# A hand-written TensorE order for the even layer's preparation, with attention one phase earlier

## The chip, the cores and the metric

The kernel runs on one core of a Trainium2 chip. The metric is device time in microseconds of one execution; the median of three timed runs stands for a kernel. A profiled execution gives the trace.

## The reference, cut to what matters

A decoder trunk of two layers: 256 positions, width 2048, float32. Only the even layer's mixer is touched here.

```python
h = x @ e_w_in                                   # even layer: one combined projection
ha, hq, hk, hv = split(h)
ya = rwkv7_mix(ha, ...)                          # A: 16 heads of 64
yb = swa_sink_attention(rot(q), rot(k), v, sinks)  # B: window 128, 16 query / 2 key heads of 64
mix = concatenate([ya, yb]) @ e_w_out
x = layer_norm(alpha * x + mix); x = layer_norm(alpha * x + swiglu(x)); x = x + sigmoid(x Wg) * (p Wp)

def rwkv7_mix(h, ...):
    h = h + (token_shift(h) - h) * mu
    r, k, v, lw, la, lg = split(h)               # widths 3 x 1024, 64, 64, 160
    decay = exp(-exp(-softplus(-(w0 + tanh(lw) @ w_up)) - 0.5))
    a = sigmoid(a0 + la @ a_up); g = sigmoid(lg) @ g_up
    kk = k * k_k / max(norm(k * k_k), 1e-12)     # per head
    # per position: state = state * w + (state @ -kk) (kk*a)^T + v k^T ;  y = state @ r
    y = groupnorm(y) * gn_w + gn_b + bonus;  return y * g

def swa_sink_attention(q, k, v, sinks):          # softmax over 128 keys back, with a sink logit per head
    e = exp(s - m); prob = e / (sum(e) + exp(sink - m)); return prob @ v
```

The odd layer (differential attention), both feed-forward blocks and the gates follow; their instructions are the same in both kernels.

## The kernel before, in words

Every product of activations and weights is three matmuls: a weight tile is read by DMA (`raw`), ACT rounds it to `hi` (L151), DVE subtracts to get `lo` (L152), and TensorE adds hi·xh, lo·xh and hi·xl into PSUM. `gemm_steps` (matmuls L178 to L180, 512 columns) yields after every six matmuls, so other work can be put between. `gemm_t` (L201 to L205, 256 columns) gives the transposed form and yields nothing.

The even mixer runs through these stages. **Preparation** (`wkv_operands`): x is transposed (L216) and split (L222, L223); a projection to 288 columns feeds the low-rank products for decay, rate and gate (L586, L590, L591, L625); then, for each half of the heads, keys and receptances are projected, and small float32 products (L633, L651, L660, L689, L697) with VectorE work in between make the recurrence operands `ar` and `bk` of all heads. From L730 to L746 VectorE inverts all 32x32 triangles of the recurrence, with two dependent instructions in each of 30 steps (L739, L741). The first value projection, `values(0, pr)`, and the attention's keys and first queries (`swa_project`) come from `gemm_steps` and lie beside the inverse. Here the Tile scheduler chooses the order on every engine.

**Phases 1 to 4** (`even_layer`): the order on TensorE is that of the program (`manual_schedule`). `weave` advances two units of the recurrence in turn, each `unit(g, c)` being four heads and half of the positions; with every link of a unit it advances the `side` work by a rate. The sides are: phase 1 `values(1, pp)`, phase 2 the second half of the queries (`swa`), phase 3 a part of the output projection with attention of head pairs 0 to 3, phase 4 another part with head pairs 4 to 7. A unit starts with four first products (L789) that are yielded as one link, each masked by VectorE into `lmat` (L790); triangular solves follow (L800 to L841); its post chain (L878 to L891) on ACT, VectorE and POOL turns `py` into the group-normed, gated result. A head pair of attention goes through scores (L964), maximum and bias on VectorE (L966), exponentials on ACT (L975), division (L980), transposes of the probabilities (L989) and the product with the values (L995). Its PSUM tiles `sx` come from a pool of two. Behind phase 4 the last output projection closes the mixer.

TensorE, VectorE and ACT each work through their own list in order; an instruction that waits holds up all that stands behind it on its engine. In phases 1 to 4 the lists of VectorE and ACT are still the Tile scheduler's.

Of the kernel before, what the change touches and what calls it, by code (L numbers as in the profile page):

```python
# [80 lines left out]

def take(steps, n):

    for _ in range(n):
        if next(steps, 0) == 0:
            return
        yield


class Trunk:  # L90
# [16 lines left out]
    def psum(self, mm, sm, sx=0):  # L107

        ctx = ExitStack()
        pool = lambda n, b: ctx.enter_context(self.tc.tile_pool(name=n, bufs=b, space=PSUM, reuse_waits="tile"))  # L110
        self.mm, self.sm = pool("mm", mm), pool("sm", sm)
        self.sx = pool("sx", sx) if sx else self.sm
        return ctx
# [70 lines left out]
    def gemm_t(self, lhs, view, n0, widths):  # L184
# [7 lines left out]
        for j, (xh, xl) in enumerate(lhs):  # L192
            hi, lo = next(ws)
            for kk in range(2):
                k = 2 * j + kk
                f0 = 0
                for i, w in enumerate(widths):
# [8 lines left out]
                                     skip_group_check=True)  # L206
        return [acc[i // 2][:w, i % 2] for i, w in enumerate(widths)]
# [203 lines left out]
def even_layer(T, a, src):  # L411
# [4 lines left out]
    with ExitStack() as ctx:  # L416
        ev = ctx.enter_context(tc.tile_pool(name="ev", bufs=1, reuse_waits="tile"))
        with tc.tile_pool(name="prep", bufs=1) as pr, T.psum(4, 4):
            ops, xT, values = wkv_operands(T, src, w_in, a, ev, pr)
            y = ops[-2]  # L420
        with tc.tile_pool(name="pairs", bufs=2, reuse_waits="tile") as pp, T.psum(2, 4, 2):
# [6 lines left out]
            swa = swa_project(T, pp, xT, w_in, a)  # L428
            qkv = next(swa)
            while next(swa) is None:  # L430
                pass
# [58 lines left out]
def wkv_operands(T, src, w_in, a, ev, pr):  # L490
    tc, nc = T.tc, T.nc
    xT = []

    def incoming():

        x = [T.res.tile([P, D], F32, name=f"x{t}") for t in range(NT)]
        for j in range(8):
# [11 lines left out]
    nc.vector.memset(vec, 0.0)  # L509
# [7 lines left out]
    nc.sync.dma_start(out=vec[50:51, 0:32], in_=mu[3328:3360].rearrange("(n p) -> n p", p=32))  # L517
    vps = T.sm.tile([P, 64], F32, name="s")
# [11 lines left out]
    early = tc.tile_pool(name="early", bufs=1)  # L530
    er = early.__enter__()
    gup0 = er.tile([P, AW], F32, name="gup0")
    gup1 = er.tile([32, AW], F32, name="gup1")
    nc.sync.dma_start(out=gup0, in_=a["e_g_up"][0][0:128])
    nc.sync.dma_start(out=gup1, in_=a["e_g_up"][0][128:160])
# [23 lines left out]
    for i in range(2):  # L559
        nc.vector.tensor_tensor(out=cum[:, i], in0=cum[:, i], in1=half, op=ALU.subtract)  # L560
# [8 lines left out]
    lg0 = er.tile([P, SEQ], F32, name="lg0")  # L569
    lg1 = er.tile([32, SEQ], F32, name="lg1")  # L570
    mix(ps[0], P, MU_L, lm)
    mix(ps[1], P, MU_L + 1, lg0)
    mix(ps[2], 32, MU_L + 2, lg1)
    nc.scalar.activation(out=lm[0:64], in_=lm[0:64], func=AF.Tanh)
    nc.scalar.activation(out=lg0, in_=lg0, func=AF.Sigmoid)
    nc.scalar.activation(out=lg1, in_=lg1, func=AF.Sigmoid)
# [3 lines left out]
    for c in range(2):  # L580
        cs = slice(c * 512, (c + 1) * 512)
        w0 = T.row(a["e_w0"][0], c * 512, 512, "brow", pr, 2)
        for t in range(NT):
            ts = slice(t * P, (t + 1) * P)
            z = T.sm.tile([P, 512], F32, name="s")
            nc.tensor.matmul(z, lm[0:64, ts], ups[0:64, cs], start=True, stop=True)  # L586
            nc.vector.tensor_tensor(out=sig[t][:, cs], in0=z, in1=w0, op=ALU.add)
            nc.scalar.activation(out=sig[t][:, cs], in_=sig[t][:, cs], func=AF.Sigmoid)
            g = T.sm.tile([P, 512], F32, name="s")
            nc.tensor.matmul(g, lg0[:, ts], gup0[:, cs], start=True, stop=False)  # L590
            nc.tensor.matmul(g, lg1[:, ts], gup1[:, cs], start=False, stop=True)  # L591
            nc.scalar.copy(out=gate[t][:, cs], in_=g)
    early.__exit__(None, None, None)
    T.rotary_tables(a["positions"][0])


    late = tc.tile_pool(name="late", bufs=1, reuse_waits="tile")
    lt = late.__enter__()
# [6 lines left out]
    for b in range(4):  # L605
        nc.vector.tensor_copy(out=m32[32 * b:32 * b + 32], in_=mtri[32 * b:32 * b + 32, 32 * b:32 * b + 32])
# [6 lines left out]
    ft = lambda n: lt.tile([P, SEQ], F32, name=n, bufs=4)  # L613
    bs = [ev.tile([P, AH], F32, name=f"bs{t}") for t in range(NT)]
    for c in range(2):
        k, kk, av, rks = [], [], [], []
        ps = T.gemm_t(xT, w_in, AW + c * 512, [128] * 4)
        for i in range(4):
            k.append(ft("k"))
            mix(ps[i], P, MU_K + 4 * c + i, k[i])  # L620
        ss = T.sm.tile([8, SEQ], F32, name="s")
        for i in range(4):
# [3 lines left out]
            av.append(ft("a"))  # L626
            nc.scalar.activation(out=av[i], in_=pa, func=AF.Sigmoid, bias=col[:, A0 + f:A0 + f + 1])
            kk.append(ft("kk"))
            nc.vector.tensor_scalar(out=kk[i], in0=k[i], scalar1=col[:, KK + f:KK + f + 1], scalar2=None,
                                    op0=ALU.mult)  # L630
            sq = lt.tile([P, SEQ], F32, name="sq")
            nc.scalar.activation(out=sq, in_=kk[i], func=AF.Square)
            nc.tensor.matmul(ss, sel[:, i], sq, start=i == 0, stop=i == 3)  # L633
        inv = lt.tile([8, SEQ], F32, name="inv")
        s0 = lt.tile([8, SEQ], F32, name="s0")
        s1 = lt.tile([8, SEQ], F32, name="s1")
        nc.vector.tensor_scalar(out=s1, in0=ss, scalar1=1e-30, scalar2=None, op0=ALU.max)
        nc.scalar.activation(out=s0, in_=s1, func=AF.Sqrt)
        nc.vector.reciprocal(out=inv, in_=s0)
        nc.vector.tensor_tensor(out=inv, in0=inv, in1=s1, op=ALU.mult)  # L640
        nc.vector.tensor_tensor(out=s0, in0=s0, in1=inv, op=ALU.add)
        nc.vector.tensor_scalar(out=s0, in0=s0, scalar1=0.5, scalar2=1e-12, op0=ALU.mult, op1=ALU.max)
        nc.vector.reciprocal(out=inv, in_=s0)

        pr_ = T.gemm_t(xT, w_in, c * 512, [128] * 4)
        for i in range(4):
            f = 4 * c + i
            r = lt.tile([P, SEQ], F32, name="r", bufs=2)
            mix(pr_[i], P, MU_R + f, r)
            pi = T.sm.tile([P, SEQ], F32, name="s")  # L650
            nc.tensor.matmul(pi, selT[:, i], inv, start=True, stop=True)  # L651
            bv = lt.tile([P, SEQ], F32, name="b", bufs=2)
# [6 lines left out]
            for t in range(NT):  # L659
                nc.tensor.matmul(pc[:, t], sig[t][:, f * P:(f + 1) * P], cum, start=True, stop=True)  # L660
# [236 lines left out]
def swa_project(T, pool, xT, w_in, a):  # L897
# [32 lines left out]
    for c in range(2):  # L930
# [16 lines left out]
        if c == 0:  # L947
            yield True
# [295 lines left out]
```

## Time and profile before

| quantity | value |
|---|---|
| median of three runs | 2599.96 us (2599.18 to 2602.28) |
| profiled execution, its span | 2597.83 us, 2595.9 us |
| mean granted TensorE clock | 0.993 of full |
| VectorE, ACT busy | 57%, 44% of the span |
| even mixer up to the last attention | 0 to 474.8 us of the span |

Busy time overlaps between instructions of one engine that are pipelined, so the length of a stretch is taken from starts and not from a sum of lengths. [...] The stages of the table of rows below were cut at the first matmul behind the x transposes (10.65 us), the end of the low-rank projection (33.5), the start of the inverse (199), and the first products of the phases.

### The profile page before, as it was taken

The page shows a single profiled execution, that of the slowest core. Times are in us where ns is not written, and L with a number is a line of the kernel's source. Part 1 is how long each engine was busy: PE and PEld are TensorE (multiplying, and loading weights), DVE is VectorE, ACT ScalarE, POOL GpSimd, SP SyncE. Part 2 cuts the span into 40 slices and gives each one's busy share as a digit, 9 for nine tenths or more (in the row PEclk, how much of TensorE's full clock was granted, in tenths as well). Part 3 has the DMA queues.
Part 4 walks back from the last instruction along what each step waited for, and adds up shares of the span by engine and source line. Part 5 has one row for each costly group of instructions (what it writes and reads, how often), then busy time and mean ns, then how long its engine had stood idle before and what let it go on. Part 6 is the DMA issues. An engine that isn't in the chain of part 4 may idle for free.

```text
span 2595.9 us, 32573 instructions
## 1 busy us (share of the span) xinstructions
PE 2541.7 (98%) x12509; PEld 2083.3 (80%) x12509; DVE 1478.8 (57%) x2144; ACT 1140.3 (44%) x1508; POOL 60.3 (2%) x126
## 2 busy tenths in 40 slices
PE   8999989999999999999999999999999999999999
PEld 6887766778888888888888888887888888888877
DVE  4668556774544454455756666657454444445574
ACT  5563344444444344443444444435444334444343
POOL 0002110000000000000000000000000000000000
PEclk9999989999999999999999999999999999999999
DMA  6445322666666666666666555557666666666654
GB/s 190 129 119 170 106 66 74 199 208 190 187 190 191 194 197 187 189 189 192 201 193 193 170 171 168 165 171 220 193 187 188 193 194 194 187 189 188 193 179 159
DMA packets 240858, 458.56 MB, mean 177 GB/s; under 512 B 15345, under 2 KB 21155, under 8 KB 240703
## 3 DMA queue, kind: packets, MB, share of 16 engines
q1 hardware_dynamic: 240702, 456.48, 58.2%
q8 instruction: 98, 1.61, 0.2%
q14 instruction: 58, 0.47, 0.1%
HBM read 453.28 MB, written 2.10 MB: 175 GB/s over the span
## 4 chain that ended last, share of the span: by engine, by line
PE 90%; DVE 5%; ACT 1%; DMA 1%; issue 1%; POOL 0%; SPq 0%; DVEq 0%; ACTq 0%; POOLq 0%
PE acc L178 27%; PE acc L180 26%; PE acc L179 26%; PE acc L201 1%; PE acc L205 1%; PE acc L203 1%; DVE lo L152 1%; PE s L216 1%; DVE lmat L790 1%; ACT hi L151 0%; PE s L806 0%; PE s L1090 0%; PE s L1118 0%; DMA lnb<-in_ln_b_dram 0%; DMA raw<-in_e_w_in_dram 0%
## 5 line engine op out<-in xcount | busy, mean ns | idle before, releaser
L152 DVE TENSOR_TENSOR lo<-raw,hi 128x1024 fp32r<-128x1024 f32 (+1 forms) x840 | 1018.4, 1214 | 936.9 <-ACT hi L151 935.7
L151 ACT CAST hi<-raw 128x1024 fp32r<-128x1024 f32 (+1 forms) x840 | 875.3, 1043 | 1196.5 <-PE acc L180 1073.6
L178 PE MATMUL acc<-hi,x0h 128*128 128x512 f32 (+1 forms) x292 | 119.8, 410 | 1.8 <-ACT x L923 0.8
L180 PE MATMUL acc<-hi,x0l 128*128 128x512 f32 (+1 forms) x292 | 117.3, 402 | 0.0
L178 PE MATMUL acc<-hi,x1h 128*128 128x512 f32 (+1 forms) x292 | 116.6, 399 | 0.0
L179 PE MATMUL acc<-lo,x5h 128*128 128x512 f32 (+1 forms) x292 | 113.5, 389 | 2.1 <-DVE lo L152 2.1
L178 PE MATMUL acc<-hi,x6h 128*128 128x512 f32 (+1 forms) x292 | 114.4, 393 | 1.2 <-DVE x L288 1.2
L178 PE MATMUL acc<-hi,x2h 128*128 128x512 f32 (+1 forms) x292 | 115.5, 396 | 0.0
L178 PE MATMUL acc<-hi,x4h 128*128 128x512 f32 (+1 forms) x292 | 115.5, 396 | 0.0
L179 PE MATMUL acc<-lo,x0h 128*128 128x512 f32 (+1 forms) x292 | 115.4, 395 | 0.0
L178 PE MATMUL acc<-hi,x5h 128*128 128x512 f32 (+1 forms) x292 | 115.3, 395 | 0.0
L179 PE MATMUL acc<-lo,x3h 128*128 128x512 f32 (+1 forms) x292 | 113.7, 389 | 1.4 <-DVE lo L152 1.3
L178 PE MATMUL acc<-hi,x3h 128*128 128x512 f32 (+1 forms) x292 | 115.0, 394 | 0.0
L179 PE MATMUL acc<-lo,x4h 128*128 128x512 f32 (+1 forms) x292 | 113.6, 389 | 1.4 <-DVE lo L152 1.4
L179 PE MATMUL acc<-lo,x6h 128*128 128x512 f32 (+1 forms) x292 | 113.5, 389 | 1.4 <-DVE lo L152 1.4
L180 PE MATMUL acc<-hi,x1l 128*128 128x512 f32 (+1 forms) x292 | 114.6, 393 | 0.0
L179 PE MATMUL acc<-lo,x2h 128*128 128x512 f32 (+1 forms) x292 | 113.9, 390 | 0.4 <-DVE lo L152 0.4
L178 PE MATMUL acc<-hi,x7h 128*128 128x512 f32 (+1 forms) x292 | 114.0, 391 | 0.0
L179 PE MATMUL acc<-lo,x1h 128*128 128x512 f32 (+1 forms) x292 | 113.9, 390 | 0.0
L180 PE MATMUL acc<-hi,x2l 128*128 128x512 f32 (+1 forms) x292 | 113.9, 390 | 0.0
L180 PE MATMUL acc<-hi,x3l 128*128 128x512 f32 (+1 forms) x292 | 113.7, 390 | 0.0
L180 PE MATMUL acc<-hi,x4l 128*128 128x512 f32 (+1 forms) x292 | 113.5, 389 | 0.0
(571 smaller groups left out, 5082.3 us busy)
## 6 DMA issues: line engine op xcount, KB each, us to landing
raw<-in_ffn_w_dram SPq DMA_DIRECT2D x528, 512.0 KB, 3.6
raw<-in_o_w_in_dram SPq DMA_DIRECT2D x96, 512.0 KB, 3.8
raw<-in_e_w_in_dram SPq DMA_DIRECT2D x64, 512.0 KB, 3.7
raw<-in_ple_w_gate_dram SPq DMA_DIRECT2D x64, 512.0 KB, 4.8
raw<-in_e_w_out_dram SPq DMA_DIRECT2D x32, 512.0 KB, 4.9
raw<-in_o_w_out_dram SPq DMA_DIRECT2D x32, 512.0 KB, 4.0
x<-in_x_dram SPq DMA_DIRECT2D x16, 256.0 KB, 4.4
lng<-in_ln_g_dram SPq DMA_DIRECT2D x16, 256.0 KB, 3.3
```

The lines of the kernel that those rows point to most:

```text
L151: nc.scalar.copy(out=hi, in_=raw)
L152: nc.vector.tensor_tensor(out=lo, in0=raw, in1=hi.bitcast(F32), op=ALU.subtract)
L178: nc.tensor.matmul(o, xh[:, kk, s], hi[:, kk], start=k == 0, stop=False)
L179: nc.tensor.matmul(o, xh[:, kk, s], lo[:, kk], start=False, stop=False)
L180: nc.tensor.matmul(o, xl[:, kk, s], hi[:, kk], start=False, stop=k == 2 * n - 1)
L201: nc.tensor.matmul(o, hi[:, kk, fs], xh[:, kk], start=k == 0 and i % 2 == 0, stop=False, skip_group_check=True)
L203: nc.tensor.matmul(o, lo[:, kk, fs], xh[:, kk], start=False, stop=False, skip_group_check=True)
L205: nc.tensor.matmul(o, hi[:, kk, fs], xl[:, kk], start=False, stop=k == nk - 1, skip_group_check=True)
L216: nc.tensor.transpose(ps[:, kk, t * P:(t + 1) * P], src[t][:, kk * P:(kk + 1) * P], self.ident)
L790: nc.vector.copy_predicated(lm4[:, i].rearrange("p a b -> p (a b)"), mask, pl.rearrange("p a b c -> p (a b c)"))
```

## The change

Preparation becomes a set of generators whose TensorE order is that of the program. `through` advances one projection and, after each of its steps (12 matmuls of `gemm_t_steps`, 6 of `gemm_steps`), one link of small products. Both value projections and the first queries and keys now lie in preparation; phase 1 has the second half of the queries as its side, phase 2 attention of head pairs 0 to 2, phase 3 pairs 3 to 5 beside the same part of the output projection, phase 4 pairs 6 and 7. The four first products of a unit are four links. Transposes of queries and keys are taken from a list (`late`) after a set number of side steps. The key norm is made with a power on POOL in place of a root on ACT and two reciprocals on VectorE. The values are no longer centred per head; the mean is taken off `py` in the post chain. At the start, the orders of ACT and VectorE are written out too. Some memsets and copies go from VectorE to POOL.

```diff
+def trailing(steps, late, at):
+
+    n = 0
+    while True:
+        try:
+            next(steps)
+        except StopIteration as e:
+            return e.value
+        yield
+        n += 1
+        if late and n in at:
+            late.pop(0)()
...
-    def gemm_t(self, lhs, view, n0, widths):
+    def gemm_t_steps(self, lhs, view, n0, widths, ahead=0):
...
-        for j, (xh, xl) in enumerate(lhs):
-            hi, lo = next(ws)
+        parts = []
+        for j in range(nk // 2):
+            while len(parts) < min(j + ahead + 1, nk // 2):
+                parts.append(next(ws))
+            hi, lo = parts[j]
             for kk in range(2):
+                xh, xl = lhs[j]
...
+                yield
...
-                side = values(1, pp)
-                weave([unit(0, 0), unit(1, 0)], side, 1.15)
+                side = trailing(queries(1, pp), late, (3, 6))
+                weave([unit(0, 0), unit(1, 0)], side, 0.7)
                 last(side)
-                side = swa
-                weave([unit(0, 1), unit(1, 1)], side, 1.25)
+                side = trailing(attend(range(3)), late, (3, 6))
+                weave([unit(0, 1), unit(1, 1)], side, 0.75)
...
-                side = zip_links(turned(), attend(range(4)), 2)
-                weave([unit(2, 0), unit(3, 0)], side, 1.25)
+                side = zip_links(turned(), attend(range(3, 6)), 2)
+                weave([unit(2, 0), unit(3, 0)], side, 0.75)
                 last(side)
-                side = zip_links(part([(yb, 0), (yb, 1)], (8, 10), False), attend(range(4, 8)), 0)
-                weave([unit(2, 1), unit(3, 1)], side, 1.0)
+                side = zip_links(part([(yb, 0), (yb, 1)], (8, 10), False), attend(range(6, 8)), 0)
+                weave([unit(2, 1), unit(3, 1)], side, 0.7)
...
-            yield xT[-1]
-
-    ps = T.gemm_t(incoming(), w_in, 3 * AW, [128, 128, 32])
+            yield
+
+    first, xs = T.gemm_t_steps(xT, w_in, 3 * AW, [128, 128, 32], ahead=1), incoming()
+    manual = tc.manual_schedule(engines={E.PE, E.Activation, E.DVE})
+    manual.__enter__()
+    last(take(xs, 2))
+    for j in range(6):
+        next(first)
+        next(xs)
+        next(first)
...
+            sq.append(two[:, i % 2])
+            nc.scalar.activation(out=sq[i], in_=k[i], func=AF.Square, scale=col[:, KK + f:KK + f + 1])
...
+        ss = T.sm.tile([P, NT, 8], F32, name="s")
+        for i in range(4):
+            for t in range(NT):
+                nc.tensor.matmul(ss[:, t], sq[i][:, t * P:(t + 1) * P], sel[:, i], start=i == 0 and t == 0,
+                                 stop=i == 3, skip_group_check=True)
+            yield
...
+        nc.vector.tensor_scalar(out=n, in0=ss, scalar1=1e-24, scalar2=None, op0=ALU.max)
+        nc.gpsimd.tensor_tensor(out=nf, in0=nf, in1=T.mhalf, op=ALU.pow)
...
+        at = {0: (feature, 0), 4: (feature, 1), 8: (feature, 2), 10: (blocks, 2 * c, 0), 11: (blocks, 2 * c, 1),
+              12: (feature, 3), 18: (blocks, 2 * c + 1, 0), 19: (blocks, 2 * c + 1, 1), 21: (bonus, 0), 22: (bonus, 1)}
+        for i in range(23):
+            if i in (1, 2, 3):
+                mix(ps[i], P, MU_R + 4 * c + i, r[i])
+            if i in at:
+                at[i][0](*at[i][1:])
+            yield
...
-            vm = pool.tile([P, 8], F32, name=f"vm{t}", bufs=1)
-            nc.vector.tensor_reduce(out=vm, in_=v3[t][:, h], axis=AX.X, op=ALU.add)
-            nc.vector.tensor_scalar(out=vm, in0=vm, scalar1=1.0 / HD, scalar2=None, op0=ALU.mult)
-            nc.vector.tensor_tensor(out=vs3[t][:, h], in0=v3[t][:, h],
-                                    in1=vm[:, :, None].to_broadcast([P, 8, HD]), op=ALU.subtract)
...
+    def products(name, n0):
+        done[name] = yield from T.gemm_t_steps(xT, w_in, n0, [128] * 4)
+
+    def through(main, *sides):
+        for _ in main:
+            for side in sides:
+                next(side, None)
+
+    through(products(("k", 0), AW), side)
+    last(side)
+    with tc.tile_pool(name="late", bufs=1, reuse_waits="tile") as lt:
+        ks = [keys(0, lt), keys(1, lt)]
+        os = [operands(0, lt), operands(1, lt)]
+        inv = inverse(lt)
+        last(rates(0, lt))
+        through(products(("r", 0), 0), ks[0])
+        last(ks[0])
+        through(products(("k", 1), AW + 512), os[0])
+        through(products(("r", 1), 512), os[0], ks[1])
+        last(os[0])
+        last(ks[1])
+        through(values(0, pr), os[1])
+        swa = keys_, queries, late, qkv = swa_project(T, xT, w_in, a)
+        through(values(1, pr), os[1], inv)
+        through(queries(0, pr), inv)
+        through(trailing(keys_(), late, (8, 11)), inv)
+        last(inv)
...
                     nc.tensor.matmul(pl[:, j], BK[f][s, c, j], AR[f][s, c], start=True, stop=True)
                 nc.vector.copy_predicated(lm4[:, i].rearrange("p a b -> p (a b)"), mask,
                                           pl.rearrange("p a b c -> p (a b c)"))
-            yield
+                yield
...
-            nc.scalar.copy(out=y, in_=py)
+            nc.vector.tensor_reduce(out=var, in_=py, axis=AX.X, op=ALU.add)
+            nc.vector.tensor_scalar(out=var, in0=var, scalar1=1.0 / HD, scalar2=None, op0=ALU.mult)
+            nc.vector.tensor_tensor(out=y, in0=py, in1=var[:, :, None].to_broadcast([P, G, HD]), op=ALU.subtract)
...
+            def turn(t=t, q=q):
+                pt = T.sx.tile([P, 4, P], F32, name=T.sxn)
+                qf = q.rearrange("p h d -> p (h d)")
+                for j in range(4):
+                    nc.tensor.transpose(pt[:, j], qf[:, j * P:(j + 1) * P], T.ident)
+                nc.scalar.copy(out=qT[:, c, :, t * P:(t + 1) * P], in_=pt)
+            late.append(turn)
```

The first place is ACT at the start of the program; `x0h`, `x1h` are the split transposes of x, `hi` the weight tiles. Before:

```order
L151 CAST hi<-raw 128x576 x3
L222 CAST x0h<-s 128x512
L222 CAST x1h<-s 128x512
L151 CAST hi<-raw 128x576 x2
L222 CAST x2h<-s 128x512
L222 CAST x3h<-s 128x512
```

After:

```order
L242 CAST x0h<-s 128x512
L242 CAST x1h<-s 128x512
L165 CAST hi<-raw 128x576 x2
L242 CAST x2h<-s 128x512
L165 CAST hi<-raw 128x576
L242 CAST x3h<-s 128x512
L165 CAST hi<-raw 128x576
```

The casts of x have moved ahead of the first weight casts.

The second place is TensorE at the start of phase 2 (units 0 and 1, second half of the positions; `acc` is a projection, `sx` attention, `ident,prob` a transpose of probabilities, `ident,q` one of queries). Before:

```order
L789 MATMUL s_3014<-ar0_1104,bk0_1105 128x256 x2
L789 MATMUL s_3018<-ar0_1104,bk0_1105 128x256 x2
L789 MATMUL s_3022<-ar1_1131,bk1_1132 128x256 x2
L789 MATMUL s_3026<-ar1_1131,bk1_1132 128x256 x2
L178 MATMUL acc_3030<-hi_3033,x0h_109 128x512
L179 MATMUL acc_3030<-lo_3034,x0h_109 128x512
L180 MATMUL acc_3030<-hi_3033,x0l_110 128x512
```

After:

```order
L891 MATMUL s_3165<-ar0_1128,bk0_1129 128x256 x2
L891 MATMUL s_3169<-ar2_1304,bk2_1305 128x256 x2
L1073 MATMUL sx_3178<-x1_2074,x0_2073 128x128
L1073 MATMUL sx_3181<-x1_2074,x0_2073 128x128
L891 MATMUL s_3193<-ar0_1128,bk0_1129 128x256 x2
L1073 MATMUL sx_3202<-x1_2074,x0_2073 128x256
L1073 MATMUL sx_3205<-x1_2074,x0_2073 128x256
L891 MATMUL s_3217<-ar2_1304,bk2_1305 128x256 x2
L1098 MATMUL sx_3222<-ident_75,prob_3177 128x128 x2
L891 MATMUL s_3226<-ar1_1219,bk1_1220 128x256 x2
L891 MATMUL s_3230<-ar3_1407,bk3_1408 128x256 x2
L1053 MATMUL sx_3234<-ident_75,q_3149 128x128 x4
```

The projection's matmuls between the first products are gone; scores (L1073), transposes of probabilities (L1098) and of queries (L1053) stand there, two `sx` tiles after one another.

The third place is VectorE ahead of the first attention scores (L966 before, L1075 after), at the start of phase 3 before and of phase 2 after; `lmat` is the masking of the first products, `q` the rotation of queries. Before:

```order
L890 TENSOR_TENSOR y_3348<-y_3348,ysq_3349 128x256
L401 TENSOR_TENSOR q_3370<-x1_2240 128x8x8
L891 TENSOR_TENSOR v1_1940<-y_3348,gate1_441 128x256
L152 TENSOR_TENSOR lo_3670<-raw_3668,hi_3669 128x1024
L790 COPY_PREDICATED lmat0_2226<-mask_2231,s_3395 128x512
L790 COPY_PREDICATED lmat0_2226<-mask_2231,s_3399 128x512
L790 COPY_PREDICATED lmat0_2226<-mask_2231,s_3403 128x512
L790 COPY_PREDICATED lmat0_2226<-mask_2231,s_3407 128x512
L966 ISA prob_3415,mx_3411<-sx_3416,x1_2240,sink_2241 128x128
L966 ISA mx_3411 128x1
L966 ISA prob_3415,mx_3411<-sx_3419,x1_2240,sink_2241 128x128
```

After:

```order
L892 COPY_PREDICATED lmat0_2729<-mask_2734,s_3165 128x512
L420 TENSOR_TENSOR q_3149<-x1_2074 128x8x8
L421 TENSOR_TENSOR q_3149<-x1_2074 128x8x8
L416 TENSOR_TENSOR x1_2074<-q_3157,cos_483 128x64
L417 TENSOR_TENSOR x1_2074<-q_3157,sin_482 128x64
L418 TENSOR_TENSOR x1_2074<-q_3157,cos_483 128x64
L419 TENSOR_TENSOR x1_2074<-q_3157,sin_482 128x64
L892 COPY_PREDICATED lmat1_2730<-mask_2734,s_3169 128x512
L420 TENSOR_TENSOR q_3157<-x1_2074 128x8x8
L421 TENSOR_TENSOR q_3157<-x1_2074 128x8x8
L1075 ISA prob_3177,mx_3173<-sx_3178,x1_2074,sink_2075 128x128
L1075 ISA mx_3173 128x1
```

The rotations of the second queries now stand directly ahead of the first scores' reading, and two of the eight maskings lie among them.

## Rows read from the trace of the kernel before

**Rows 1.** The page, busy time, share of the span and instructions of each engine.
```profile
PE 2541.7 (98%) x12509; PEld 2083.3 (80%) x12509; DVE 1478.8 (57%) x2144; ACT 1140.3 (44%) x1508; POOL 60.3 (2%) x126
```

**Rows 2.** Busy time by stage, the even mixer; header row first.
```profile
core 0: us, PE busy (x) PEld busy (x) DVE busy (x) ACT busy (x) POOL busy (x), PEclk, DMA share, GB/s
0.00:10.65 10.65, 2.20 (x9) 1.44 (x9) 4.01 (x6) 3.84 (x6) 4.83 (x44) 1.00 0.80 259
...
33.50:199.00 165.50, 162.38 (x1066) 134.66 (x1065) 101.88 (x183) 97.61 (x164) 0.53 (x1) 0.99 0.44 125
199.00:244.20 45.20, 39.62 (x220) 32.80 (x218) 43.75 (x100) 17.31 (x24) 13.01 (x15) 1.00 0.64 188
244.20:285.90 41.70, 41.24 (x333) 31.22 (x332) 20.83 (x42) 16.46 (x31) 9.03 (x11) 1.00 0.40 115
285.90:340.30 54.40, 46.66 (x329) 36.35 (x328) 33.40 (x72) 15.19 (x23) 8.71 (x13) 0.92 0.32 97
340.30:408.70 68.40, 61.07 (x457) 45.86 (x456) 38.14 (x127) 33.90 (x93) 5.73 (x10) 0.89 0.23 69
408.70:463.20 54.50, 49.54 (x385) 37.06 (x385) 36.79 (x119) 22.66 (x63) 1.05 (x1) 0.97 0.22 68
463.20:474.80 11.60, 10.19 (x60) 7.19 (x59) 9.83 (x27) 6.28 (x14) 1.05 (x1) 1.00 0.43 133
```

**Rows 3.** Timeline of the start: start, length, engine, line, operands, [idle before, releaser].
```profile
4.68 1.54 PE L216 MATMUL s<-ident,x 128*128 128x128 f32 x6 [0.47 <-DMA x<-in_x_dram]
...
9.44 0.67 ACT L151 CAST hi<-raw 128x576 fp32r<-128x576 f32 x1 [2.13 <-DMA raw<-in_e_w_in_dram]
...
10.65 0.58 PE L201 MATMUL acc<-x0h,hi 128*128 128x256 f32 x1 [4.43 <-ACT x0h L222]
```

**Rows 4.** TensorE timeline: a projection with small products between.
```profile
257.37 0.50 PE L178 MATMUL acc<-hi,x2h 128*128 128x512 f32 x1
...
258.17 0.39 PE L178 MATMUL acc<-hi,x2h 128*128 128x512 f32 x1
258.40 0.40 PE L179 MATMUL acc<-lo,x2h 128*128 128x512 f32 x1
...
258.96 0.62 PE L819 MATMUL s<-blk,pm 32*32 32x32 f32 x16
...
285.86 2.10 PE L789 MATMUL s<-ar,bk 64*128 64x256 f32 x16
```

**Rows 5.** Waits of TensorE, preparation: us in total, times, longest.
```profile
PE acc L179 <- DVE lo L152: 4.7, 4, 2.1
```

**Rows 6.** Waits of TensorE in phases 2, 3 and 4.
```profile
PE sx L945 <- DVE q L401: 4.5, 1, 4.5
PE s L800 <- DVE lmat L790: 2.1, 1, 2.1
...
PE sx L989 <- DVE mx L966: 5.6, 7, 2.5
...
PE sx L989 <- DVE mx L966: 5.0, 6, 1.4
```

**Rows 7.** VectorE by line, preparation: busy us, mean ns, idle before.
```profile
L152 DVE TENSOR_TENSOR lo<-raw,hi 128x1024 fp32r<-128x1024 f32 x49 | 59.8, 1224 | 40.3 <-ACT hi L151 40.3
...
L639 DVE RECIPROCAL inv<-s 8x256 f32<-8x256 f32 x2 | 3.5, 1742 | 1.0 <-ACT s L638 1.0
```

**Rows 8.** VectorE by line, phases 1 to 4.
```profile
L891 DVE TENSOR_TENSOR v<-y,gate 128x256 f32<-128x256 f32 x8 | 3.3, 416 | 0.1
```

**Rows 9.** TensorE timeline, start of phase 3.
```profile
339.32 1.09 PE L945 MATMUL sx<-ident,q 128*128 128x128 f32 x4 [4.46 <-DVE q L401]
...
349.67 0.44 PE L989 MATMUL sx<-ident,prob 128*128 128x128 f32 x2 [2.51 <-DVE mx L966]
...
355.05 0.63 PE L178 MATMUL acc<-hi,x0h 128*128 128x512 f32 x1
355.48 0.63 PE L179 MATMUL acc<-lo,x0h 128*128 128x512 f32 x1
```

More of the change, by code (lines that the diff above doesn't have):

```diff
@@ L594, in wkv_operands @@
+    side = ranks()
+    next(side)
     T.rotary_tables(a["positions"][0])
-    late = tc.tile_pool(name="late", bufs=1, reuse_waits="tile")
-    lt = late.__enter__()
+    manual.__exit__(None, None, None)
+    manual = tc.manual_schedule(engines={E.PE})
+    manual.__enter__()
     AR, BK, EW = [], [], []
@@ L612, in wkv_operands, with until, rates @@
     c2 = lambda u: u.rearrange("p (c t) -> p c t", t=P)
-    ft = lambda n: lt.tile([P, SEQ], F32, name=n, bufs=4)
     bs = [ev.tile([P, AH], F32, name=f"bs{t}") for t in range(NT)]
[L615 to L621, printed above, removed]
+    done, made = {}, {}
+    def until(name):
+        while name not in done:
+            yield
+    def rates(c, lt):
+        av = made["a", c] = []
         for i in range(4):
@@ L632, in wkv_operands @@
[L632 to L640, printed above, removed]
@@ L650, in wkv_operands, with operands, feature @@
+    def operands(c, lt):
+        yield from until(("inv", c))
+        yield from until(("r", c))
+        ps, k, av, inv = done["r", c], made["k", c], made["a", c], made["inv", c]
+        r = [lt.tile([P, SEQ], F32, name="r", bufs=4) for i in range(4)]
+        mix(ps[0], P, MU_R + 4 * c, r[0])
+        def feature(i):
+            f = 4 * c + i
             pi = T.sm.tile([P, SEQ], F32, name="s")
             nc.tensor.matmul(pi, selT[:, i], inv, start=True, stop=True)
+            pc = T.sm.tile([P, NT, 2, P], F32, name="s")
+            for t in range(NT):
+                nc.tensor.matmul(pc[:, t], sig[t][:, f * P:(f + 1) * P], cum, start=True, stop=True)
@@ L657, in wkv_operands @@
             nc.vector.tensor_tensor(out=k[i], in0=k[i], in1=av[i], op=ALU.mult)
-            pc = T.sm.tile([P, NT, 2, P], F32, name="s")
-            for t in range(NT):
-                nc.tensor.matmul(pc[:, t], sig[t][:, f * P:(f + 1) * P], cum, start=True, stop=True)
             ee = lt.tile([P, NT, 2, P], F32, name="ee", bufs=2)
@@ L680, in wkv_operands @@
             EW.append(ew)
-            if f % 2 == 0:
-                continue
-            g = f // 2
-            for par in range(2):
-                s = slice(64 * par, 64 * par + 64)
-                pl = T.sm.tile([P, 2, NT, P], F32, name="s")
-                for fi in range(2):
-                    for t in range(NT):
-                        nc.tensor.matmul(pl[:, fi, t], BK[2 * g + fi][s, t, 0], AR[2 * g + fi][s, t, 0],
-                                         start=True, stop=True)
-                for b in range(4):
-                    q = slice(32 * b, 32 * b + 32)
-                    nc.scalar.copy(out=bview[q, g, par], in_=pl[q, :, :, q])
@@ L694, in wkv_operands, with blocks @@
-        for t in range(NT):
+        def blocks(g, par):
+            s = slice(64 * par, 64 * par + 64)
+            pl = T.sm.tile([P, 2, NT, P], F32, name="s")
+            for fi in range(2):
+                for t in range(NT):
+                    nc.tensor.matmul(pl[:, fi, t], BK[2 * g + fi][s, t, 0], AR[2 * g + fi][s, t, 0],
+                                     start=True, stop=True)
+            for b in range(4):
+                q = slice(32 * b, 32 * b + 32)
+                nc.scalar.copy(out=bview[q, g, par], in_=pl[q, :, :, q])
+            done[g, par] = True
@@ L709, in values @@
         acc = yield from T.gemm_steps(xT, w_in, 2 * AW + c * 512)
-        cs, h = slice(c * 512, (c + 1) * 512), slice(8 * c, 8 * c + 8)
-        muv = T.row(mu, 2 * AW + c * 512, 512, "brow", pool, 2 - c)
+        cs = slice(c * 512, (c + 1) * 512)
+        muv = T.row(mu, 2 * AW + c * 512, 512, "brow", pool, 1)
+        vs = [ev.tile([P, 512], F32, name=f"vs{t}") for t in range(NT)]
+        nc.gpsimd.memset(vs[0][0:1], 0.0)
         for t in range(NT):
@@ L937, in swa_project @@
             T.rotate(q, t, 8, 8, rot)
[L938 to L948 removed]
+            def turn(t=t, q=q):
[4 more added lines that the diff above has]
+                nc.scalar.copy(out=qT[:, c, :, t * P:(t + 1) * P], in_=pt)
+            late.append(turn)
+    return keys, queries, late, (qT, kT, vv, bias, sink)
 def swa_attend(T, sw, fs, ybT, qT, kT, vv, bias, sink):
```

253 lines of the change are left out of this document (133 added, 120 removed).

## The prediction

> **What bounds the kernel now.** I read the page's busy line first, then the table by stage, then the waits of TensorE in each stage, then single stretches of the timeline. TensorE is busy 98% of the span [rows 1], so only its list counts: time is won where it stood idle or ran at the low clock, and lost where it gets more to do. All that changes lies before the last output projection. The stage table [rows 2] gives the idle time of TensorE there as length less busy: 8.5 us at the start, 3.1 + 5.6 = 8.7 in preparation, 0.5 in phase 1, 7.7, 7.3 and 5.0 in phases 2 to 4, 1.4 in the tail. The granted clock gives the rest: 2 x 0.08 x 54.4 = 8.7 us at the lower level in phase 2, 2 x 0.11 x 68.4 = 15 in phase 3, 3.3 in phase 4. A matmul of a projection follows the one before after 0.23 us at the high level and 0.43 at the low [rows 4, 9], so these 27 us cost up to 13 us. Idle time and clock of the phases, some 34 us, are the stake.
>
> What the waits are: in preparation the largest is for `lo` of VectorE, 4.7 us [rows 5]; that engine is busy 43.75 of 45.2 us there [rows 2], because of the inverse. In phase 2 TensorE stands 4.5 us for the rotated queries, and 2.1 us for a masked first product; in phases 3 and 4 it stands 5.6 and 5.0 us for probabilities, released by VectorE [rows 6].
>
> **The change part by part**, each against the profiled execution (2597.83 us).
>
> *Start: -2.4 us.* The x transposes that the first product needs end at about 4.68 + 1.54 = 6.2, yet the first matmul starts at 10.65, because ACT has three weight casts ahead of `x0h` and the third waits 2.13 us for its DMA [rows 3]. With the two casts of x first, at most 0.67 us each (the length of the cast in the row), and one weight cast behind them, the first matmul starts at 6.2 + 3 x 0.67 = 8.2. Bounds: 0 if the weights, not the casts, set the pace of the first ten matmuls; -3.
>
> *Preparation: +17 us.* `values(1)` comes in: 16 steps of six, 96 matmuls at 0.23 = +22. Its eight weight tiles stay behind the same DMA queue (share 0.44 and 0.64 of the engines here [rows 2]), and are asked for in the new order; I cost that at nothing, and if a tile came late it would be a wait of one to two us. The first products of the first unit, 16 matmuls, leave for phase 1: -2.1, the length of such a group [rows 4]. Small products now stand at 41 places between projection matmuls, where I counted 26. Six matmuls between two such places take 258.96 - 257.37 = 1.59, where six in a row take 1.38 [rows 4], so a place costs 0.2 and 15 more cost +3. Idle time: VectorE loses the reciprocals (3.5 us a line [rows 7], two lines) and the centring, and its inverse now spreads over three projections instead of two. The `lo` tiles of `values(1)` add 8 x 1.22 = 9.8 us [rows 7]. VectorE's work over that stretch I sum to 54 us against 54 us of TensorE: a balance, so I let half the idle time go, 8.7 to 4: -4.7. The low clock in the first part (2 x 0.01 x 165.5 = 3.3 us) costs up to 1.7, say -1. Sum 22 - 2.1 + 3 - 4.7 - 1 = +17. Bounds: idle all gone +13; idle as before and each `lo` of `values(1)` waited for, +31.
>
> *Power on POOL, memsets on POOL, table loads on ACT: 0.* The norm has a stretch of eight steps between its parts; POOL is busy 13 of 45 us, ACT 97.6 of 165.5 [rows 2]. Without that cover each half of the keys would wait some 2 us, and could not gain more than the reciprocals' 3.5.
>
> *Phase 1: +2.3.* 16 steps of a projection as before, plus the 2.1 of first products and one more place: 41.7 to 44. It had 0.5 us of idle time, so nothing can be won; one by one, the first products need less of VectorE at a time, and that hides nothing here.
>
> *Phase 2: -10.9.* Out go 16 steps of 1.59 = 25.4 us. What is left of 46.66 busy, less those and half of the 8.7 us at low clock, is 46.66 - 25.4 - 4.4 = 17 for two units and the query transposes. In come three head pairs. One pair: phase 4's 49.54 busy, less 1.6 for the low clock, 25.4 for its projection and 15 for its units (17 less two groups of query transposes of about 1 us, as in [rows 9]), leaves 7.5 for the three pairs that lie in it, 2.5 each; I take 2.8, since without a projection a group more often starts from a stop: 3 x 2.8 = 8.4. Work: 26 us at the high level. Beside it stand waits that a projection used to fill. At the phase's start VectorE works off the post chains of two units (seven operations of 0.42 us each [rows 8], two of them new, and some short ones), twelve operations of the rotations and the first maskings before it reads the first scores; TensorE has two `sx` tiles and then stands. Walking both lists I get about 5.5 us for the tiles, 4 us for the first probabilities, 4.5 us later: 14. Behind the waiting transposes stands all else of the list, both units too. After each such stop the clock falls as it does in phase 3, where TensorE stood 4.46 and 2.51 us and matmuls then followed each other after 0.43 us [rows 9]; 7 us of that level cost 3.5. Sum 26 + 14 + 3.5 = 43.5 instead of 54.4. Bounds: 36 (waits of 10, no low clock) and 54 (below).
>
> [...]
>
> *Phase 3: -4; phase 4: -6.5; tail: -2.3.* Phase 3 has one head pair fewer (-2.8), and part of its idle time and low clock (7.3 + 7.5), but it again begins with post chains ahead of scores: -1.2 for that. Phase 4 has two pairs fewer, 5.6, and with them some of its 5.0 us of waits: -0.9. In the tail the last attention (about 1 us, and a wait of 1.4 by the idle time [rows 2]) no longer stands before the transposes of the last units. The mean taken off `py` lengthens the post chain by three VectorE operations less one ACT copy, about 1 us; it is hidden in the phases, and at the tail, where TensorE waits for the last chain, could cost 1.
>
> **Sum.** -2.4 + 17 + 2.3 - 10.9 - 4 - 6.5 - 2.3 = -6.8: 2591.0 for a profiled execution. The median of the timed runs lies 2.1 above the profiled one, so 2593.
>
> **Rivals.**
>
> *Stalls move to phase 2, no change.* VectorE's backlog and the low clock hold phase 2 at its 54 us: 26 us of work at the low level throughout is 52. Then 10.9 is not won: 2593 + 10.9 = 2604. For it: without a projection, every link of attention is a round of TensorE, VectorE, ACT, VectorE, and only two units fill it. Against it: phase 4 ran at 0.97 with four pairs. It decides if the phase's granted clock is under 0.65 or it lasts over 50 us.
>
> *Slower: preparation stalls on VectorE.* The fixed order puts `lo` of `values(1)` behind the inverse's dependent operations; before, the scheduler gave TensorE other work. Place: L193 behind L166 in the last 60 us of preparation. Price: idle stays at 8.7 and the eight `lo` tiles, 9.8 us, come on top, 18.5 instead of 4: +14.5, 2593 + 14.5 = 2608. For it: 43.75 of 45.2 busy, 4.7 us of waits already. Against: 54 to 54 is a balance, and the centring and reciprocals are gone. It decides from 12 us of idle time there.
>
> *A larger gain.* The fewer attention links per phase, first products spread, and shorter queues leave little idle: phase 2 at 36 (-7.5), phases 3 and 4 another -5, preparation without idle time -3: 2593 - 15.5 = 2578. For it: the stake of 34 us is large. Against: the dependent chain at each phase's start remains in the lists.
>
> **How the numbers follow.** My forecast 0.45, the larger gain 0.25, no change 0.15, slower 0.15. A change within 0.2% (5.2 us, about what a measurement here can tell) is 2594.8 to 2605.2. The forecast, 2593 give or take 6, is faster in two thirds and else the same; so faster 0.30 + 0.25 = 0.55, same 0.15 + 0.14 = 0.29, slower 0.16. The range reaches to the middle of the larger gain and to the edge of the slower case, 2577 to 2606; the forecast's own is 2586 to 2600.
>
> **What would show it.** First matmul of the low-rank product near 8.2; the first products of phase 1 near 244 + 15 = 259; phase 1 44 us long, phase 2 43.5 with waits for `sx` tiles and for probabilities at its start, phase 3 64, phase 4 48. Idle time of preparation near 4. The forecast is wrong if phase 2 is under 38 or over 50, if preparation is idle for over 12, or if anything behind the mixer changes.

## The result, and the profile after

The changed kernel is slower: 2615.56 us median (four runs, 2610.2 to 2619.9) against 2601.12 (2599.18 to 2604.47), ratio 1.0056, interval 1.0044 to 1.0068. The forecast was 2593, range to 2606. The profiled execution took 2619.90, 22.1 more than that of before, and so lies at the upper end; its first transpose behind the mixer starts at 543.05 instead of 521.90, and what follows takes the same time in both to 0.8 us. So 21 of the 22 us are lost in the mixer. Its stages, with the columns of [rows 2]:

```profile
0.00:8.14 8.14, 2.20 (x8) 1.43 (x9) 2.20 (x3) 3.08 (x5) 7.17 (x52) 1.00 0.71 215
...
30.30:199.00 168.70, 168.70 (x1106) 143.92 (x1105) 95.79 (x173) 99.31 (x164) 6.82 (x4) 1.00 0.49 146
199.00:251.75 52.75, 51.78 (x284) 44.70 (x282) 48.05 (x110) 22.68 (x31) 3.67 (x6) 1.00 0.57 153
251.75:298.19 46.44, 46.44 (x349) 35.06 (x348) 27.61 (x59) 16.62 (x30) 11.74 (x20) 1.00 0.44 138
298.19:353.38 55.19, 43.76 (x311) 33.61 (x310) 31.09 (x124) 15.75 (x53) 7.17 (x13) 0.68 0.07 20
353.38:432.64 79.26, 73.76 (x432) 52.73 (x430) 36.25 (x112) 29.68 (x77) 4.28 (x9) 0.73 0.16 47
432.64:485.32 52.68, 47.47 (x355) 35.26 (x355) 34.94 (x92) 17.33 (x43) 1.11 (x1) 0.97 0.38 121
```

Preparation ends 7.55 us later, with the 22 us of the second value projection more to do and 2 us of first products less: its 8.7 us of idle time [rows 2] are 1.0. The phases lose it: +4.7, +0.8, +10.9 and -1.8 us; what follows to the end of the mixer gives 1.0. Phase 3 is the odd one: a head pair fewer, only 5.5 us of idle time (7.3 before), and 11 us longer. The granted clock says why. Read in stretches of 2 us over phases 2 and 3 of both kernels, it is 1.00 or 0.50, and something between only where it changes; a projection's matmuls follow one another after 0.23 us at 1.00 and after 0.43 at 0.50 [rows 4, 9]. A mean of 0.68 over 55.19 us is thus 2 x 0.32 x 55.19 = 35 us at the low level in phase 2, and 2 x 0.27 x 79.26 = 43 in phase 3, 78 against 24 before. Two long spells make up 72 of it (same columns):

```profile
303.40:334.10 30.70, 27.04 (x163) 20.17 (x164) 14.52 (x56) 7.08 (x25) 0.00 (x0) 0.51 0.06 18
347.80:388.80 41.00, 34.98 (x105) 23.39 (x106) 19.34 (x63) 8.57 (x26) 1.11 (x1) 0.51 0.09 26
```

In the second spell TensorE is busy for 35 of 41 us and the clock stays at 0.51. The timeline of TensorE there (start, length, line, operands, count):

```profile
374.20 0.63 PE L193 MATMUL acc<-lo,x0h 128*128 128x512 f32 x1
374.62 0.63 PE L194 MATMUL acc<-hi,x0l 128*128 128x512 f32 x1
...
378.76 2.07 PE L891 MATMUL s<-ar,bk 64*128 64x256 f32 x4
380.76 0.79 PE L192 MATMUL acc<-hi,x1h 128*128 128x512 f32 x1
...
384.68 2.07 PE L891 MATMUL s<-ar,bk 64*128 64x256 f32 x4
```

Six matmuls of a projection, 0.43 us apart as in [rows 9], then small products with first products among them (L891, 64 rows of the array), then six again. The clock rose at 388.8, 2 us behind the last of these first products; in phase 2 it rose 14 us behind the last one (which ended at 320.4), so this alone does not time it. Before, the first products were over when the projection began, and the spell that began at 351.9 ended after 10 us.

The waits of TensorE, those of phase 2 first, then of phase 3:

```profile
PE sx L1098 <- DVE prob L1089: 6.3, 2, 3.8
PE sx L1073 <- DVE mx L1075: 3.6, 1, 3.6
...
PE sx L1098 <- DVE mx L1075: 2.0, 4, 0.6
PE sx L1098 <- DVE prob L1089: 1.6, 1, 1.6
```

They are no longer than forecast, and those of phase 3 are shorter than in [rows 6].

### The profile page after: what moved, and what is told of

It reads as the page before. It is cut to its first block, busy times and chain, and to the rows that moved or that the text cites. A ratio compares the mean times of both kernels' runs of the same rounds, so it can differ in the third digit from the quotient of the medians.

```text
span 2617.8 us, 32595 instructions
## 1 busy us (share of the span) xinstructions
PE 2571.3 (98%) x12529; PEld 2110.5 (81%) x12529; DVE 1469.2 (56%) x2131; ACT 1135.5 (43%) x1496; POOL 61.8 (2%) x138
## 4 chain that ended last, share of the span: by engine, by line
PE 93%; DVE 4%; DMA 1%; ACT 1%; issue 1%; POOL 0%; SPq 0%; DVEq 0%; ACTq 0%; POOLq 0%
PE acc L192 27%; PE acc L194 26%; PE acc L193 26%; PE acc L220 2%; PE s L891 1%; PE acc L222 1%; PE acc L224 1%; PE s L236 1%; DVE lo L166 1%; PE s L908 0%; PE s L1199 0%; PE s L1227 0%; PE sx L1104 0%; DMA lnb<-in_ln_b_dram 0%; PE sx L1073 0%
## 5 line engine op out<-in xcount | busy, mean ns | idle before, releaser
L166 DVE TENSOR_TENSOR lo<-raw,hi 128x1024 fp32r<-128x1024 f32 (+2 forms) x840 | 1018.5, 1214 | 937.5 <-ACT hi L165 936.0
L165 ACT CAST hi<-raw 128x1024 fp32r<-128x1024 f32 (+2 forms) x840 | 876.9, 1045 | 1179.8 <-PE acc L194 1065.2
L194 PE MATMUL acc<-hi,x5l 128*128 128x512 f32 (+1 forms) x292 | 113.9, 390 | 0.0
```

Source lines behind the costliest of these rows:

```text
L165: nc.scalar.copy(out=hi, in_=raw)
L166: nc.vector.tensor_tensor(out=lo, in0=raw, in1=hi.bitcast(F32), op=ALU.subtract)
L194: nc.tensor.matmul(o, xl[:, kk, s], hi[:, kk], start=False, stop=k == 2 * n - 1)
```

## The experiments

All times are medians beside the kernel before run on the same chip (2600.8 to 2601.1). "One by one" and "grouped" speak of a unit's four first products, "the low level" of the time at a granted clock of 0.50, worked out as above.

**1. Grouped again.**

```diff
-                yield
+            yield          # rates 0.7 -> 1.0, 0.75 -> 1.07
```

> Undoes one part: the four first products of a unit are one link again, with the side rates raised (0.7 to 1.0, 0.75 to 1.07) so that the sides keep their pace. Theory C (phase 2 without a projection drops TensorE to its low clock, and phase 3 starts in it): the time stays that of the changed kernel, 2615 give or take 5, with over 60 us at the low level in phases 2 and 3 together. Rival O (the first products, put one by one between projection steps, keep the clock low in phase 3): phase 3 falls from 79 to about 65 us, total about 2602.

2595.06, ratio 0.9978 (0.9967 to 0.9989): 20 us less than the changed kernel, and faster than before. My first theory, that it is the missing projection of phase 2, fell here. Phases 2 to 4:

```profile
299.70:349.05 49.35, 38.45 (x311) 30.49 (x310) 31.29 (x126) 15.29 (x53) 7.25 (x13) 0.74 0.11 32
349.05:409.42 60.37, 53.78 (x433) 41.57 (x431) 34.98 (x112) 29.27 (x77) 5.94 (x10) 0.96 0.16 50
409.42:459.30 49.88, 46.12 (x355) 34.79 (x355) 34.47 (x89) 17.55 (x43) 0.00 (x0) 0.97 0.42 132
```

Phase 3 loses 19 us at slightly more idle time (6.6 us); the low level of phases 2 and 3 falls from 78 to 30 us.

**2. The new preparation with the old phases.**

```diff
-                side = trailing(queries(1, pp), late, (3, 6))
+                side = trailing(values(1, pp), late, (3, 6))     # grouped, rate 1.15
-                side = trailing(attend(range(3)), late, (3, 6))
+                side = queries(1, pp)                            # then attend(range(4)), attend(range(4, 8))
-        through(values(1, pr), os[1], inv)
-        through(queries(0, pr), inv)
+        through(queries(0, pr), os[1], inv)
```

> Keeps the new preparation, without the second value projection, and undoes the new phases: values in phase 1, queries in phase 2, attention of pairs 0 to 3 in phase 3 and 4 to 7 in phase 4, first products grouped, the rates of before. Theory C: the preparation by itself is a gain. It ended at 251.75 with a projection of 22 us more and 2 us of first products less than before, which ended at 244.2, so it saves 22 - 2 - 7.5 = 12 us; phases 2 to 4 return to 54, 68 and 55 us; total 2601 - 12 = 2589. Rival P (the new order of operands and the longer post chain cost something in the phases as well): 2595 to 2605, with phases 2 to 4 longer than before by several us each.

2601.30, ratio 0.9995 (0.9986 to 1.0003). Preparation ended at 229.3, the 15 us that it should, and the phases gave all of it back: 53.5, 53.0, 76.4 and 56.5. Phase 1 begins with this wait, for VectorE, which is still behind from the inverse:

```profile
PE s L890 <- DVE lmat L891: 8.1, 1, 8.1
```

Phase 1 is 11.8 us longer than before [rows 2], 2 of them first products that came from preparation, and phase 3 is 8.0 longer; phase 2 is 1.4 shorter and phase 4 2.0 longer. So rival P has the total, but not the place, which it saw in each of phases 2 to 4. With one projection more in preparation, as in the changed kernel, VectorE has time to catch up: phase 1 there has no idle time.

**3. More work in phase 2.**

```diff
-                side = trailing(attend(range(3)), late, (3, 6))
+                side = filled(trailing(attend(range(3)), late, (3, 6)), 3)   # 3 matmuls 128x512 per link
```

> The changed kernel with three more matmuls (128 x 512, of x by itself, into a PSUM tile that nothing reads) at each of the 18 links of attention in phase 2: 54 matmuls, 12.4 us of work at 0.23 each, and no other change. Theory C: the clock stays high, phase 2 is no longer than its 55 us (about 48: 26 of work, 12.4 of filler, 10 of waits), phase 3 falls to about 65; total 2615 - 7 - 14 = 2594, in spite of more work. Rival S (the wait chain through VectorE and ACT sets phases 2 and 3, the clock only follows): phase 2 stays at 55 or grows, phase 3 stays at 79, total 2615 to 2627.

2617.31, ratio 1.0070 (1.0049 to 1.0090): no help. The profiled execution is the slowest of five (2629.59, 12 us above the median). In it phase 2 grew to 67.6 us, its idle time shrank from 11.4 to 4.6 us, and the clock stayed low:

```profile
296.86:364.44 67.58, 62.98 (x365) 44.46 (x364) 30.23 (x121) 16.48 (x54) 6.48 (x13) 0.70 0.05 16
364.44:439.75 75.31, 68.78 (x431) 49.34 (x431) 36.83 (x114) 29.32 (x76) 4.93 (x10) 0.82 0.16 49
```

So in this execution more work and less idle time went with 41 us at the low level in phase 2, where the changed kernel has 35; phase 3 had 27 instead of 43. It is not typical, though: its mean granted clock over the whole span is 0.983, that of the other four 0.987 to 0.990, and that of the changed kernel 0.983 to 0.986. From 0.9835 to 0.989, the medians, the low level is some 29 us shorter, worth up to 14 us, about what the filler's own 12.4 us cost. That more work shortens the low level is thus not excluded. Rival S had the total and the growth of phase 2, not the reason: the waits that it names had shrunk.

**4. A projection in every phase.**

```diff
-                side = trailing(queries(1, pp), late, (3, 6))
+                side = trailing(queries(0, pp), late, (3, 6))
-                side = trailing(attend(range(3)), late, (3, 6))
+                side = mixed(queries(1, pp), attend(range(3)), 3)
-        through(queries(0, pr), inv)
```

> The changed kernel with a projection in every phase: the first queries go from preparation to phase 1, the second queries to phase 2, beside attention of pairs 0 to 2, whose first scores wait for the transposes of the first queries there; the rest as in the changed kernel (split tiles of the attention's and the recurrence's results change places). Theory C: low clock under 20 us in phases 2 to 4; preparation ends near 252 - 25 + 2 for less cover of the inverse = 229, phase 1 46, phase 2 26 + 25 + 8 = 59, phase 3 64, phase 4 50, so the last output projection starts some 30 us earlier than in the changed kernel: 2585. Rival S: phases 2 and 3 keep the waits of the changed kernel on top of the projection: phase 2 over 70, phase 3 79, total over 2610.

2614.88, ratio 1.0049 (1.0035 to 1.0062), phases 57.9, 68.7, 68.1 and 54.1: a miss by 30 us. The low level of phases 2 to 4 is 34 us instead of under 20, and phase 1 waits 6.4 us for a masking, as in 2. Rival S had the total, but not the phases, which it saw at over 70 and 79.

**5. One by one in the kernel before.**

```diff
-            yield
+                yield          # rates 0.8, 0.875, 0.875, 0.7
```

> The kernel before with one part of the change alone: the first products of a unit one by one (rates 1.15, 1.25, 1.25, 1.0 lowered to 0.8, 0.875, 0.875, 0.7 to keep the pace of the sides). Theory D (spread over a phase, the first products lie between the pieces of projection that would otherwise raise the clock again, so a low spell lasts longer; not a matter of waits): the low level in phases 2 to 4 grows from 27 us to 50 or more, total 2601 + 10 = 2611, idle time of the phases no larger. Rival W (it costs only where a phase has no projection, as phase 2 of the changed kernel): total within 3 us of 2601.

2610.87, ratio 1.0034 (1.0022 to 1.0047). The total is as theory D had it, the mechanism is not: phases 2 to 4 have 17 us at the low level, less than before, and are 3 us longer together; 9.9 us were lost ahead of phase 2, which starts at 295.80 instead of 285.9, part of it in low spells of the preparation (17 us instead of 3), whose order the scheduler had changed. The mean granted clock of all five executions is 0.992 or 0.993, within the 0.990 to 0.995 of the kernel before, so most of the 10 us is not the clock. In phase 2, at a granted clock of 1.00, a single first product stands like this between pieces of the projection:

```profile
299.31 1.13 PE L789 MATMUL s<-ar,bk 64*128 64x256 f32 x4
300.37 0.50 PE L178 MATMUL acc<-hi,x0h 128*128 128x512 f32 x1
```

Its four matmuls take 1.06 us, where 16 in a row take 2.10 [rows 4], so 0.53 for four. For the 32 of a phase that would be up to 4 us of TensorE's own time (an estimate from these two rows). How much of the 10 us it makes up was not measured.

**6. One by one in phase 1 only.**

```diff
-                yield
+                if i == 3 or (g < 2 and c == 0):
+                    yield
```

> The changed kernel with the first products one by one only in phase 1 and grouped in phases 2 to 4 (rates there 1.07, 1.07, 1.0). Theory D: phases 2 to 4 as with all grouped, 49, 60 and 50 us, phase 1 46.5 instead of 48.5 since one by one spares it the wait for a masking: total 2593. Rival W (phase 1 takes no harm, phase 2 does, and phase 3 only inherits its clock): the same total, but then a low spell that begins in phase 2 reaches as far into phase 3 as in the changed kernel, to 389 us, total 2605.

2591.59, ratio 0.9973 (0.9961 to 0.9985); phases 45.7, 49.3, 60.5 and 49.9, as forecast by theory D. The low spell of phase 2 takes 5 us of phase 3 (0.96 of 60.46), so rival W falls. In phase 1, at a granted clock of 1.00 and without idle time, one by one did no harm here; in the kernel before it cost 10 us at an undisturbed mean clock (experiment 5).

**7. First products over 128 rows.**

```diff
-  nc.tensor.matmul(pl[:, j], BK[f][s, c, j], AR[f][s, c], start=True, stop=True)
+  nc.tensor.matmul(pl[:, j], BK[f][:, c, j], AR[f][:, c], start=True, stop=True)
```

> The changed kernel with each first product contracting over all 128 rows of its operands instead of the 64 of its head; the results of two heads are then mixed, and the output is not the reference's; number, length and order of instructions stay. Theory D1 (the half-used array of the first products is what keeps the clock low): low level in phases 2 and 3 falls from 78 us to under 45, total about 2600. Rival D2 (any small products between the pieces do it, however many rows they use): low level 70 us or more, total 2612 to 2618.

2596.16, ratio 0.9981 (0.9971 to 0.9992): 19 us less than the changed kernel, at the same list of instructions and about the same idle time (10.8 and 6.4 us in phases 2 and 3, 11.4 and 5.5 in the changed kernel).

```profile
296.23:347.98 51.75, 40.99 (x311) 32.04 (x310) 30.94 (x124) 15.61 (x53) 7.10 (x13) 0.74 0.07 21
347.98:413.27 65.29, 58.90 (x432) 44.16 (x431) 35.91 (x112) 29.50 (x77) 4.28 (x9) 0.94 0.19 57
```

The low level of the two phases falls from 78 to 27 + 8 = 35 us. It is not one execution's luck: the mean granted clock is 0.990 to 0.994 in all eleven, 0.983 to 0.986 in the four of the changed kernel. Theory D1 holds, for these products in this place.

**8. The same with zeros.**

```diff
+  nc.gpsimd.tensor_copy(out=wide[key][s], in_=BK[2 * g + i // 2][s, c])   # other half zero
-  nc.tensor.matmul(pl[:, j], BK[f][s, c, j], AR[f][s, c], start=True, stop=True)
+  nc.tensor.matmul(pl[:, j], w[:, j], AR[f][:, c], start=True, stop=True)
```

> The changed kernel, all first products one by one, with the result kept: in phases 2 to 4 the stationary operand of a head is copied by POOL into a tile of 128 rows whose other half is zero, so that each first product again contracts over 128 rows, now with nothing but zeros in the added ones. Theory D1a (what counts for the clock is how many rows an instruction uses): as with 128 rows of data, low level in phases 2 and 3 about 35 us, total 2596 to 2600. Rival D1b (what counts is data that change in the array): zeros do not help, low level stays near 78 us and the total at 2612 to 2618.

2598.87, ratio 0.9996 (0.9986 to 1.0006): 17 us less, with the result kept. Phases 2 and 3:

```profile
296.76:345.74 48.98, 37.29 (x311) 28.33 (x309) 31.42 (x124) 15.57 (x53) 10.63 (x21) 0.83 0.07 22
345.74:411.03 65.29, 58.90 (x433) 44.22 (x431) 35.92 (x112) 29.47 (x77) 7.60 (x17) 0.94 0.19 57
```

25 us at the low level, and a mean granted clock of 0.989 to 0.993 in the eleven executions. So zeros do as well as data.

**9. Zeros, with the first products grouped after phase 1.** Experiments 6 and 8 together.

> The kernel with the first products one by one in phase 1 only, and the copies with a zero half in phases 2 to 4. Theory D1a: the spell of 27 us at the low level in phase 2 gets shorter, but the first products are over in the first 10 us of a phase there, so by little: 2585 to 2592. Rival D1b: 2592, or a few us more for POOL's copies if a phase waits for one.

2594.81, ratio 0.9978 (0.9968 to 0.9987): nothing gained on experiment 6. That is outside the range of theory D1a and within the rival's, although experiment 8 had spoken against the rival: the low level of phases 2 and 3 is 24 + 13 us, where experiment 6 has 26 + 5, and a few waits for maskings (1.6 us) came in.

**10. Experiment 4 with the first products one by one in phase 1 only.**

> The kernel with a projection in every phase (first queries in phase 1, second queries in phase 2 beside attention of pairs 0 to 2), with the first products one by one in phase 1 only. It was at 2615 with all of them one by one. Theory D: low level in phases 2 to 4 under 25 us; the phases 58, 62, 60 and 50 us, total 2595 to 2600, the waits of 6.4 us in phase 1 and 6.1 in phase 2 remaining. Rival W: 2615 stays, since a projection was in every phase already.

2603.80, ratio 1.0007 (0.9998 to 1.0016). 11 us less than 4, all of it behind phase 2 (62.6 and 49.7 instead of 68.1 and 54.1); the low level of phases 2 to 4 is 28 us, over the 25 expected and only 6 less than in 4, so the clock accounts for some 3 of the 11 us. The waits of 6.4 and 6.7 us remain, and the total is 4 us above theory D's range.

**11. Half of the second queries in each of phases 1 and 2,** on top of experiment 6.

```diff
-                side = trailing(queries(1, pp), late, (3, 6))
+                rest = queries(1, pp)
+                side = trailing(take(rest, 8), late, (3, 6))     # rate 0.4
-                side = trailing(attend(range(3)), late, (3, 6))
+                side = mixed(rest, attend(range(3)))             # one step at every second link
```

> The kernel with the first products one by one in phase 1 only, and the projection of the second queries halved: 8 steps in phase 1, 8 in phase 2, one beside every second link of attention. Phase 1 had no idle time with 16 steps. Theory: phase 1 takes 46 - 12.5 = 33 us, or some more if it now waits; phase 2 has 26 + 12.5 us of work and fewer waits and less low clock, 48 instead of 49; total 2591.6 - 12 = 2580. Rival: phase 1 waits with half the cover (38 or more), phase 2 keeps its 11 us of waits and its 27 us at the low level on top (62): 2592 to 2600.

2584.64, ratio 0.9939 (0.9924 to 0.9953): the best version, faster than both kernels.

```profile
250.79:286.52 35.73, 34.32 (x301) 26.34 (x301) 20.56 (x48) 11.63 (x24) 11.38 (x20) 0.95 0.40 134
286.52:341.34 54.82, 46.87 (x351) 35.32 (x350) 38.24 (x136) 19.31 (x57) 8.93 (x14) 0.86 0.16 48
```

Phases 1 and 2 together take 90.6 us instead of 95.0; phase 2 has 15 us at the low level instead of 26. Phase 3 took 3 us more. The theory had 33 and 48 us for phases 1 and 2, the rival 38 or more and 62: the outcome lies between, nearer to the theory.

## Why the prediction was wrong

- **Start:** -2.5 us against -2.4. Right.
- **Preparation:** +10 against +17. The balance on VectorE was read too darkly: 1.0 us of idle time instead of 4. Most of the other 4 us is TensorE's own work, which grew by 18.5 us (168.70 + 51.78 against 162.38 + 39.62 busy) where my terms sum to 22; which of them was too large I cannot say.
- **Power and memsets on POOL:** no wait of TensorE for them shows. Right.
- **Phase 1:** +4.7 in the profiled execution, forecast +2.3, without idle time and at a clock of 1.00: what is missing is work. I had costed the first products as 16 in a row and one more place of 0.2 us; one by one, a link of four takes about twice as long as four in a row (1.06 us against 0.53, experiment 5).
- **The step that failed** is the one that costed the first products one by one: "one by one, the first products need less of VectorE at a time, and that hides nothing here". It was weighed in phase 1 alone, at nothing, and not at all in phases 2 to 4. Undone, it is worth 20 us of the median (experiment 1), most of it in phase 3, for which I had forecast -4 and which grew by 10.9.
- **Phase 2:** 55.2 against 43.5. The waits were right (11.4 us for 14), the work too; the low clock was mis-sized, 35 us instead of 7. Some 26 us of these remain with the first products grouped (0.74 of 49.35), so that the term would have been three to four times too small in any case; the rest, and phase 3, came from one by one.
- **Phase 4 and tail:** -1.8 and -1.0 against -6.5 and -2.3. Phase 4 is 49.9 with the products grouped, so 3 of the 5 us missing belong to the same step.
- **The rival that named the low clock in phase 2** had its price (54; it took 55.2) and its sign of over 50 us, yet its total, 2604, is 12 us short, since it too stopped at the end of that phase. The low level went on into phase 3, beside a projection, where my -4 had taken part of it off. The rival's 52 us take all of phase 2 at the low level, which no run shows: in the changed kernel it was 35 of 55 us. The slower rival, a stall in preparation, did not occur; the larger gain neither.

With the products grouped the time, 2595, comes near the forecast of 2593, but partly by luck. Against the forecast the start of phase 1 is 7.6 us earlier, phase 3 gains 4 more, phases 1 and 2 together are 10.4 worse and phase 4 is 1.9 worse.

Shown: in the changed kernel the order one by one costs 20 us (experiment 1), and the same order costs only 1 to 4 us over grouped when its products use all rows, with data or zeros (7 and 8). Not shown: what the granted clock follows, why grouped first products over all rows gain nothing (9), what ends a spell in a phase that has none of them left, and why the same order does not lengthen the low level of the kernel before (5).

## What to carry to other kernels

When small products are threaded between the matmuls of a long projection, read the granted clock of that stretch and not only its idle time: phase 3 here had less idle time than before (5.5 us against 7.3) and took 11 us more. Where that clock is low, as in phases 2 and 3 here (0.68 and 0.73), it is worth trying to bunch products that contract over half of the array (20 us, experiment 1), or to pad them with zeros to all rows (17 us, experiment 8); in phase 1 strewing them took a wait of 1.7 us away, at a clock of 1.00 (experiments 1 and 6), but it cost 10 us in the kernel before (experiment 5). A gain in one stage has to be followed to the next: preparation ended 15 us earlier in experiment 2, but 8 us came back as a wait for VectorE at the start of phase 1, and phase 3 grew by 8.

## What the runs showed of the hardware

- From 347.8 us of the changed kernel on, the granted clock of TensorE stayed at 0.51 for 41 us while it was busy 35 of them, among others with 23 matmuls of 128 x 512 (phase 2 of the profiled execution of experiment 3 has 63 of 67.6 us busy at a mean of 0.70).
- In phases 2 and 3 of the changed kernel, with the same list of instructions, first products over 128 rows instead of 64 left 35 us at the low level instead of 78 (experiment 7); with zeros in half of the rows, copied there by POOL, it was 25 (experiment 8). Grouped behind phase 1, they gained nothing by it (37 us in experiment 9 against 31 in experiment 6).
- Four matmuls of a first product between pieces of a projection took 1.06 us at a granted clock of 1.00 (experiment 5), four of 16 in a row 0.53 [rows 4].
